# Where TensorE's tiles begin: stationary tiles moved to several distances, modulo 512 bytes, from their moving partners

## The chip, the cores and the metric

The kernel runs on one core of one Trainium2 chip. The metric is the device time of the whole launch in microseconds (us), the median of several runs. TensorE multiplies, VectorE (DVE), ScalarE (ACT) and GpSimd (POOL) do the elementwise work, SyncE (SP) and ScalarE's queue issue most transfers, and 16 DMA engines move the data.

## What is computed

One block of an encoder for 512 tokens of width 1024, in float32. A mixer comes first, then a retrieval layer over 16,384 experts, then a norm. Cut to what matters:

```python
h = rmsnorm(x, g_mix); z = h @ w_in
a = pool_mixer(z_pool) @ w_branch_pool
b = short_conv_mixer(z_c, z_b, z_v) @ w_branch_conv
x = x + (sigmoid(gate_a) * a + sigmoid(gate_b) * b) @ w_out
h2 = rmsnorm(x, g_ffn); q = h2 @ w_q
# per token and head: the best 16 of 128 x 128 sums of two key scores, softmax over the 16
act = gelu(expert_u[idx] . h2)
x = x + sum_k gate_k * act_k * expert_v[idx_k]
out = rmsnorm(x, g_final)
```

## The kernel before, in words

Every product of TensorE is made of three matmuls: each float32 operand is split into a high part (rounded to the `F32R` type, by ScalarE) and a low part (the rest, by VectorE or GpSimd), and high times high, high times low and low times high are summed (`mm3`, lines 57 to 60). Each matmul has its own load of 128 x 128 stationary elements, which TensorE makes while the matmul before it streams its moving operand.

The stages follow one another. **Mixer**: `w_in` comes in 16 pieces of 1 MB (`w_load`, line 181; tile `raw`), each is split into `wh` and `wl` in the pool `wpool`, and multiplies `hH` and `hL`, the normed and transposed input (`z_part`, line 210); then the branches and `w_out`. **Queries and keys**: eight heads (`queries`, `best_keys`, `top16`), with VectorE finding the best keys. **Expert gates**: for 320 of the 512 tokens the layer is computed densely, for all 128 blocks of 128 experts: `u_mm` (line 453) multiplies one block's `uH` and `uL` (stationary) with `h2H` and `h2L` (moving, 320 columns) in 24 matmuls; blocks 0 to 75 are done ahead, beside the queries and beside the building of a gate matrix from one-hot tiles `oi` and `oj` (line 865), which goes through memory (`Gd`, from the tile `stage`). The other tokens gather their experts' rows one by one (`gather`, tile `gr`), two VectorE passes over each. **Values**: for each block `weigh` (line 886) multiplies the activations (`a`, or `ab` when they come back from memory) with the gates `gt` and splits the result into `wH` and `wL`, and `v_part` (line 905) uses these as stationary operands against the moving `vH` and `vL`, in 18 matmuls of 512 columns; the last 52 blocks do their `u_mm` in the same loop (lines 966 to 990).

The order is written out by hand, and tiles stand in SBUF where pools put them: a pool's tiles stand one behind the other in the order in which they are first asked for, left pools upwards, right ones (`side="right"`) downwards. Tile sizes alone thus set the byte in a partition at which each tile begins. In the kernel before, all that TensorE reads begins at a multiple of 512 bytes: `hH`, `hL` (and `h2H`, `h2L`, which take their place), `uH`, `uL`, `vH`, `vL`, `wH`, `wL`, `wh`, `wl`, `mH`, `mL`, `oi`, `oj`. Slices of them along a partition (`wH[:, ts]`, `uH[:, c]`) step by whole multiples of 512 bytes too. The gates `gt[:, :, k]` of the four blocks of one load, read by VectorE and ScalarE, begin 128 bytes apart. Three lines show how a tile's size serves this:

```python
warm = edge.tile([P, 120], F32, name="warm")
rank0 = keep.tile([P, 48], F32, name="rank0")[:, :TOPK]
us[i] = [upool.tile([P, DC, P], F32R, tag=f"u{x}{i % 3}", name=f"u{x}", bufs=1) for x in "HL"]
```

`u_load`, `u_high` (lines 435 to 443) keep three blocks of u in turn (`i % 3`), `weigh` three of `wH` and of `wL`.

Of the kernel before, what the change touches and what calls it, by code (L numbers as in the profile page):

```python
# [8 lines left out]
F32 = mybir.dt.float32  # L9
F32R = mybir.dt.float32r  # L10
I32 = mybir.dt.int32
U32 = mybir.dt.uint32
# [4 lines left out]
P = 128  # L17
D = 1024
T = 512
NT = T // P  # L20
DC = D // P
H = 8
TOPK = 16
# [7 lines left out]
TD = KD * P  # L31
# [16 lines left out]
def block_kernel(ctx: ExitStack, tc: tile.TileContext, io, out, dbg=None):  # L48
# [27 lines left out]
        work.tile([P, 5, 1], F32, tag="rms", name="st", bufs=3)  # L76
    keep = ctx.enter_context(tc.tile_pool(name="keep", bufs=1))
    edge = ctx.enter_context(tc.tile_pool(name="edge", bufs=1, side="right"))
    warm = edge.tile([P, 120], F32, name="warm")
    pscale = keep.tile([P, 4], F32, name="pscale")  # L80
    cw = keep.tile([P, 12], F32, name="cw")
    rank0 = keep.tile([P, 48], F32, name="rank0")[:, :TOPK]
# [236 lines left out]
    for hf in range(2):  # L319
        us = []  # L320
# [25 lines left out]
        for e in range(2):  # L346
            zb = z_chunk(wb, e)
            p = fpool.tile([P, T], F32, tag="p", name="yb", bufs=2)
# [10 lines left out]
    for hf in range(4):  # L359
# [14 lines left out]
        for e in range(2):  # L374
# [3 lines left out]
            m = fpool.tile([P, T], F32, tag="p", name="m", bufs=2)  # L378
            t = fpool.tile([P, T], F32, tag="s", name="t", bufs=2)
# [44 lines left out]
    upool = tc.alloc_tile_pool(name="upool", bufs=2, reuse_waits="tile")  # L424
    qpool = tc.alloc_tile_pool(name="qpool", bufs=1, reuse_waits="tile")
# [6 lines left out]
    raws, us, hid = {}, {}, {}  # L432
    nu = [0]

    def u_load(i):
        if i < NK:
            raws[i] = upool.tile([P, DC, P], F32, tag=f"ur{i % 3}", name="ur", bufs=1)
            nc.sync.dma_start(raws[i], io["expert_ut"][i])

    def u_high(i):  # L440
        if i < NK:
            us[i] = [upool.tile([P, DC, P], F32R, tag=f"u{x}{i % 3}", name=f"u{x}", bufs=1) for x in "HL"]
            nc.scalar.copy(us[i][0], raws[i])  # L443

    def u_low(i, eng):
# [3 lines left out]
    def u_split(i, eng):  # L449
        u_high(i)  # L450
        u_low(i, eng)
# [18 lines left out]
    def u_tick(n=1, eng=nc.gpsimd, half=None):  # L470
        for _ in range(n):
            i = nu[0]
            nu[0] += 1
            u_load(i + 3)
            u_high(i + 2)
            if eng is not None:
                u_low(i + 2, eng)
            u_act(i, u_mm(i, half))
# [12 lines left out]
    for i in range(3):  # L491
        u_load(i)
# [16 lines left out]
    nc.sync.dma_start(skT, io["sub_keys_t"])  # L509

    nc.vector.tensor_scalar(rank0, iota[:, :TOPK], 2.0, 1.0, op0=ALU.mult, op1=ALU.max)
    ones = qpool.tile([P, NT * TOPK], U32, name="ones")
    nc.vector.memset(ones, 1)
    thirty = qpool.tile([P, NT * TOPK], U32, name="thirty")
    nc.vector.memset(thirty, 30)
# [314 lines left out]
    for n in range(0, TD // 4, 2):  # L830
# [14 lines left out]
        i = nu[0]  # L845
        nu[0] += 1
        u_load(i + 3)
        u_high(i + 2)
        one_hots(n + 2)
        one_hots(n + 3)  # L850
# [24 lines left out]
    epool = tc.alloc_tile_pool(name="epool", bufs=2, reuse_waits="tile")  # L875
# [10 lines left out]
    def weigh(i):  # L886

        if i < NK:
            a = abs_.pop(i) if i < n_ahead else hid.pop(i)
            g = gts.pop(i)  # L890
            gu = g[:, :TU // TG]
            nc.vector.tensor_tensor(gu, a.rearrange("p (n t) -> p n t", t=TG), gu, ALU.mult)  # L892
            wH = epool.tile([P, TD], F32R, tag="wH", name="wH", bufs=3)
            wL = epool.tile([P, TD], F32R, tag="wL", name="wL", bufs=3)
            nc.scalar.copy(wH.rearrange("p (n t) -> p n t", t=TG), g)  # L895
            ws[i] = (wH, wL, g)
# [52 lines left out]
    for k in range(U_END):  # L949
        u_tick(1, nc.vector)  # L950
        gather(n_done[0] + 2, 2)
        if k == 0:
            v_high(0)
            v_low(0)
        if k == 1:
            v_high(1)
            v_low(1)
        if k == U_END - 2:
            weigh(0)
            weigh_low(0)  # L960
# [5 lines left out]
    for i in range(NK - 1):  # L966
# [14 lines left out]
        if i < NK - 3:  # L981
            v_mm(i)
        weigh(i + 1)
        first = n_done[0] + 1
        for k in range(n_done[0], want):
# [85 lines left out]
```

## Time and profile before

| | |
|---|---|
| runs shown | 1512.49, 1513.56, 1513.67 us; median 1513.56 us |
| profiled execution | 1516.77 us, its span 1515.0 us, mean granted TensorE clock 0.993 |
| TensorE matmul busy | 1465.3 us, 97% of the span |
| TensorE weight load busy | 1291.0 us, 85% |
| VectorE busy | 1223.0 us, 81% |
| ScalarE, GpSimd busy | 668.8 and 653.8 us, 44% and 43% |
| DMA | 415.72 MB, mean 274 GB/s |

Busy time is the union of the durations that the trace gives. The end of a matmul is modelled, so that successive matmuls overlap in it: their rate is read from the distance between their starts, not from their durations. An instruction's "idle before" is the time for which its engine had nothing running, with the event that ended it. The granted clock is in parts of the higher of TensorE's two levels.

### The profile page before, as it was taken

The numbers are of one execution on the slowest core, as the hardware profiler recorded it, in microseconds if no ns is written. First come the engines' busy times: TensorE is split into PE (matmuls) and PEld (weight loads), VectorE is DVE, ScalarE is ACT, GpSimd is POOL, SyncE is SP. The second block draws the span as 40 slices with busy tenths as digits, with TensorE's granted clock in tenths as the row PEclk, the third lists the DMA queues.
The fourth block names the chain that finished last, engine by engine and source line by source line (L and its number), as shares of the span: only waits on it lengthen the run. The fifth ranks groups of instructions, "written<-read, shape, count | busy, mean of one in ns | idle before, by whom it ended". The sixth has DMA issues, their size and how long they took to land.

```text
span 1515.0 us, 22211 instructions
## 1 busy us (share of the span) xinstructions
PE 1465.3 (97%) x7953; PEld 1291.0 (85%) x7953; DVE 1223.0 (81%) x2399; ACT 668.8 (44%) x1144; POOL 653.8 (43%) x432
## 2 busy tenths in 40 slices
PE   8999999999998999999999999999999999999997
PEld 6788888788897989898997788888889999999996
DVE  5842434659999899999988888888889999999975
ACT  4323223423333677776853334333343343334334
POOL 3433333247772454544243243332345655555510
PEclk9999999999999999999999999999999999999999
DMA  5222224432224899999999999999999999999951
GB/s 188 83 98 83 97 87 159 125 130 102 110 74 136 301 392 363 373 376 387 363 323 396 346 352 377 363 349 376 360 376 368 381 393 364 405 375 380 372 221 70
DMA packets 163358, 415.72 MB, mean 274 GB/s; under 512 B 13744, under 2 KB 80304, under 8 KB 156848
## 3 DMA queue, kind: packets, MB, share of 16 engines
q1 hardware_dynamic: 102992, 210.99, 38.7%
q0 software_dynamic: 46144, 167.80, 28.9%
q10 hardware_dynamic: 14112, 35.53, 6.0%
q8 instruction: 62, 1.02, 0.3%
q14 instruction: 48, 0.39, 0.1%
HBM read 376.05 MB, written 37.62 MB: 273 GB/s over the span
## 4 chain that ended last, share of the span: by engine, by line
PE 66%; DVE 24%; issue 4%; DMA 4%; ACT 2%; POOL 0%; DVEq 0%; ACTq 0%; SPq 0%; POOLq 0%
PE b L911 30%; PE b L60 11%; PE b L59 11%; PE b L58 11%; DVE gr L731 5%; DMA ab<-Ad 3%; DVE uL L447 2%; DVE oj L812 2%; DVE oi L812 2%; PE b L865 1%; DVE oj L823 1%; DVE key L610 1%; DVE eq L596 1%; DVE sc L530 1%; DVE ti L528 1%
## 5 line engine op out<-in xcount | busy, mean ns | idle before, releaser
L60 PE MATMUL b<-h2H,uL 128*128 128x320 f32 x1024 | 321.7, 314 | 19.1 <-DVE uL L447 18.7
L58 PE MATMUL b<-h2H,uH 128*128 128x320 f32 x1024 | 322.5, 315 | 0.2 <-ACT h2H L54 0.2
L59 PE MATMUL b<-h2L,uH 128*128 128x320 f32 x1024 | 317.9, 310 | 0.9 <-DVE h2L L55 0.9
L719 POOL DMA_INDIRECT gr<-in_expert_u,gidx x128 | 172.7, 1349 | 242.8 <-DVE dots L731 147.6
L719 POOL DMA_INDIRECT gr<-in_expert_v,gidx x128 | 164.9, 1288 | 199.5 <-DVE x L736 119.8
L911 PE MATMUL b<-vH,wH 128*128 128x512 f32 x768 | 238.5, 391 | 5.2 <-ACT wH L895 5.2
L911 PE MATMUL b<-vH,wL 128*128 128x512 f32 x768 | 238.2, 391 | 0.0
L911 PE MATMUL b<-vL,wH 128*128 128x512 f32 x768 | 237.5, 390 | 0.0
L60 PEld LDWEIGHTS b<-h2H,uL 128*128 128x128 f32 x1024 | 193.7, 189 | 27.7 <-DVE uL L447 27.7
L880 ACT CAST vH<-vr 128x1024 fp32r<-128x1024 f32 x128 | 134.7, 1052 | 172.3 <-PE b L911 120.0
L884 DVE TENSOR_TENSOR vL<-vr,vH 128x1024 fp32r<-128x1024 f32 x128 | 156.7, 1224 | 60.1 <-ACT vH L880 59.4
L59 PEld LDWEIGHTS b<-h2L,uH 128*128 128x128 f32 x1024 | 194.0, 189 | 3.1 <-DVE h2L L55 1.2
L58 PEld LDWEIGHTS b<-h2H,uH 128*128 128x128 f32 x1024 | 194.2, 190 | 2.5 <-ACT h2H L54 0.5
L911 PEld LDWEIGHTS b<-vH,wL 128*128 128x128 f32 x768 | 143.2, 188 | 32.5 <-DVE wL L902 2.8
L911 PEld LDWEIGHTS b<-vL,wH 128*128 128x128 f32 x768 | 144.2, 188 | 30.8
L911 PEld LDWEIGHTS b<-vH,wH 128*128 128x128 f32 x768 | 141.5, 188 | 33.6 <-ACT wH L895 7.6
L736 DVE SCALAR_TENSOR_TENSOR x<-gr,dots,x 128x1024 f32<-128x1024 f32 x128 | 163.8, 1280 | 1.0
L731 DVE CUSTOM_DVE_ANT_0 gr<-gr,hn 128x1024 f32<-128x1024 f32 x128 | 153.8, 1218 | 2.0 <-DMA gr<-in_expert_u,gidx 2.0
L443 ACT CAST uH<-ur 128x1024 fp32r<-128x1024 f32 x128 | 133.9, 1047 | 35.4 <-ACT a L464 19.6
L447 DVE TENSOR_TENSOR uL<-ur,uH 128x1024 fp32r<-128x1024 f32 x113 | 139.5, 1236 | 8.1 <-ACT uH L443 8.1
L55 POOL TENSOR_TENSOR wl<-raw,wh 128x2048 fp32r<-128x2048 f32 (+1 forms) x21 | 79.5, 3784 | 150.6 <-ACT wh L54 150.6
L895 ACT CAST wH<-gt 128x384 fp32r<-128x384 f32 x128 | 65.8, 514 | 175.3 <-DVE gt L892 175.3
(216 smaller groups left out, 2487.3 us busy)
## 6 DMA issues: line engine op xcount, KB each, us to landing
ur<-in_expert_ut SPq DMA_DIRECT2D x128, 512.0 KB, 7.1
vr<-in_expert_v SPq DMA_DIRECT2D x128, 512.0 KB, 6.6
Gd<-stage ACTq DMA_DIRECT2D x22, 1024.0 KB, 9.0
gt<-Gd SPq DMA_DIRECT2D x32, 704.0 KB, 9.5
raw<-in_w_in SPq DMA_DIRECT2D x15, 1024.0 KB, 4.8
Ad<-a ACTq DMA_DIRECT2D x76, 160.0 KB, 5.7
ab<-Ad SPq DMA_DIRECT2D x76, 160.0 KB, 8.1
raw<-in_w_q SPq DMA_DIRECT2D x8, 1024.0 KB, 6.7
```

The source lines that it names most:

```text
L55: (nc.gpsimd if pool else nc.vector).tensor_tensor(Ld, src, f(Hd), ALU.subtract)
L58: nc.tensor.matmul(o, lh, rh, start=first, stop=False)
L59: nc.tensor.matmul(o, lh, rl, start=False, stop=False)
L60: nc.tensor.matmul(o, ll, rh, start=False, stop=last)
L443: nc.scalar.copy(us[i][0], raws[i])
L447: eng.tensor_tensor(us[i][1], raws.pop(i), f(us[i][0]), ALU.subtract)
L719: nc.gpsimd.indirect_dma_start(out=r, out_offset=None, in_=io["expert_u" if kind == "u" else "expert_v"], in_offset=bass.IndirectOffsetOnA ...
L731: nc.vector.tensor_tensor_reduce(out=r, in0=r, in1=src, op0=ALU.mult, op1=ALU.add, scale=1.0, scalar=0.0, accum_out=dst)
L736: nc.vector.scalar_tensor_tensor(x1[:, KD + g], r, dots[:, g, k:k + 1], x1[:, KD + g], op0=ALU.mult, op1=ALU.add)
L880: nc.scalar.copy(vs[i][0], vraw[i])
L884: nc.vector.tensor_tensor(vs[i][1], vraw.pop(i), f(vs[i][0]), ALU.subtract)
L911: nc.tensor.matmul(acc[tb][hf], lw[:, ts], rw[:, hf * 512:(hf + 1) * 512], start=i == 0 and rw is vH and lw is wH, stop=last and i == NK - 1)
```

## The change

Six tiles get other sizes or places, and nothing else changes. A helper `room` gives a u tile some elements behind its 1,024, which moves the tiles behind it: `ur` of the third block, `uL` of the first and of the second are 64, 64 and 128 bytes longer. `wH` is 320 bytes longer than its 384 elements. `ones`, 256 bytes, leaves `qpool` for the pool `edge` at the right end, where `warm` shrinks from 480 to 32 bytes: the right pools move by 192 bytes.

```diff
-    warm = edge.tile([P, 120], F32, name="warm")
+    warm = edge.tile([P, 8], F32, name="warm")
+    ones = edge.tile([P, NT * TOPK], U32, name="ones")
...
+    def room(tag, name, dt, more):
+
+        t = upool.tile([P, D + more], dt, tag=tag, name=name, bufs=1)
+        return t[:, :D].rearrange("p (c m) -> p c m", c=DC)
+
     def u_load(i):
         if i < NK:
-            raws[i] = upool.tile([P, DC, P], F32, tag=f"ur{i % 3}", name="ur", bufs=1)
+            raws[i] = room(f"ur{i % 3}", "ur", F32, 16 if i % 3 == 2 else 0)
             nc.sync.dma_start(raws[i], io["expert_ut"][i])
...
-            us[i] = [upool.tile([P, DC, P], F32R, tag=f"u{x}{i % 3}", name=f"u{x}", bufs=1) for x in "HL"]
+            us[i] = [room(f"u{x}{i % 3}", f"u{x}", F32R, (16, 32, 0)[i % 3] if x == "L" else 0) for x in "HL"]
             nc.scalar.copy(us[i][0], raws[i])
...
-    ones = qpool.tile([P, NT * TOPK], U32, name="ones")
     nc.vector.memset(ones, 1)
...
-            wH = epool.tile([P, TD], F32R, tag="wH", name="wH", bufs=3)
+            wH = epool.tile([P, TD + 80], F32R, tag="wH", name="wH", bufs=3)[:, :TD]
```

Where the tiles begin, in bytes modulo 512, as the two programs place them, and the distance from the moving to the stationary one (all were 0 before, but for `a`):

| tile | after | its partner in TensorE, after | distance |
|---|---|---|---|
| `uH`, `uL`, blocks 0, 1, 2 of three | 64, 128, 256 | `h2H`, `h2L`: 0 | 64, 128, 256 |
| `wH`, three buffers | 256, 64, 384 | `vH`, `vL`: 256 | 0, 320, 128 |
| `wL`, three buffers | 192 | `vH`: 256 | 448 |
| `wh`, `wl` (and `raw`) | 192 | `hH`, `hL`, `h2H`, `h2L`, `pH`, `yH`: 0; in `w_out` they move against `mH`, `mL`: 0 | 192; 320 |
| `oi`, `oj` | 256 | each other | 0 |
| `skT` | 256 | `q`: 0 | 256 |
| `gr`, `vr`, `gt`, `ab` (0 before) | 256 | not read by TensorE | |
| `stage` (0 before) | 192 | not read by TensorE | |
| `a`, three buffers (0, 256, 0 before) | 256, 0, 256 | not read by TensorE | |

On all five engines the instructions stand in the same order as before, with the same waits, but for one place on VectorE, at the beginning of the queries (`thirty` is a second table of constants, `tv` the best scores). Before:

```order
L511 TENSOR_SCALAR rank_73<-iota 128x16
L513 MEMSET ones 128x64 [waits Pool_49]
L515 MEMSET thirty 128x64
L526 MAX tv<-sc 128x8 [waits Activation_49]
```

and with the change, where the lines' numbers are higher by four or five:

```order
L517 TENSOR_SCALAR rank_74<-iota 128x16
L518 MEMSET ones 128x64
L520 MEMSET thirty 128x64 [waits Pool_49]
L531 MAX tv<-sc 128x8 [waits Activation_49]
```

The wait for GpSimd moved from the first constant to the second, which stands right behind it.

## Rows read from the trace of the kernel before

**Rows 1.** The page: span, and busy time, share and instructions of each engine.

```profile
span 1515.0 us, 22211 instructions
PE 1465.3 (97%) x7953; PEld 1291.0 (85%) x7953; DVE 1223.0 (81%) x2399; ACT 668.8 (44%) x1144; POOL 653.8 (43%) x432
```

**Rows 2.** Stretches of the span, busy time and instructions of each engine.

```profile
core 0: us, PE busy (x) PEld busy (x) DVE busy (x) ACT busy (x) POOL busy (x), PEclk, DMA share, GB/s
0.00:300.00 300.00, 289.83 (x1324) 237.15 (x1324) 146.49 (x193) 100.72 (x125) 102.40 (x39) 0.99 0.33 112
300.00:500.00 200.00, 188.25 (x1064) 170.53 (x1065) 175.72 (x900) 71.75 (x107) 114.91 (x74) 0.97 0.32 116
500.00:800.00 300.00, 282.00 (x2033) 272.90 (x2031) 287.30 (x492) 212.70 (x498) 138.76 (x91) 0.99 0.97 366
800.00:1100.00 300.00, 298.54 (x1305) 243.65 (x1306) 250.51 (x350) 117.77 (x166) 99.15 (x86) 1.00 1.00 364
1100.00:1400.00 300.00, 300.00 (x1652) 271.21 (x1652) 277.34 (x352) 119.22 (x172) 171.63 (x124) 1.00 1.00 380
1400.00:1515.00 115.00, 106.64 (x580) 95.59 (x578) 85.69 (x117) 46.65 (x77) 26.98 (x20) 0.98 0.59 223
```

**Rows 3.** The chain that ended last, by engine and by line.

```profile
PE 66%; DVE 24%; issue 4%; DMA 4%; ACT 2%; POOL 0%; DVEq 0%; ACTq 0%; SPq 0%; POOLq 0%
PE b L911 30%; PE b L60 11%; PE b L59 11%; PE b L58 11%; DVE gr L731 5%; DMA ab<-Ad 3%; DVE uL L447 2%; DVE oj L812 2%; DVE oi L812 2%; PE b L865 1%; DVE oj L823 1%; DVE key L610 1%; DVE eq L596 1%; DVE sc L530 1%; DVE ti L528 1%
```

**Rows 4.** Timeline of TensorE in the mixer: start, duration, instruction.

```profile
149.77 0.39 PE L58 MATMUL b<-hH,wh 128*128 128x512 f32 x1
...
152.95 0.39 PE L60 MATMUL b<-hH,wl 128*128 128x512 f32 x1
```

**Rows 5.** Timeline of TensorE in the values stage, two matmuls a row.

```profile
899.75 0.62 PE L911 MATMUL b<-vL,wH 128*128 128x512 f32 x2
900.21 0.62 PE L911 MATMUL b<-vH,wL 128*128 128x512 f32 x2
...
902.92 0.62 PE L911 MATMUL b<-vH,wL 128*128 128x512 f32 x2
```

**Rows 6.** Timeline of matmuls (PE) and weight loads (PEld) in one block of u.

```profile
1205.82 0.31 PE L59 MATMUL b<-h2L,uH 128*128 128x320 f32 x1
1205.82 0.19 PEld L60 LDWEIGHTS b<-h2H,uL 128*128 128x128 f32 x1
...
1205.97 0.31 PE L60 MATMUL b<-h2H,uL 128*128 128x320 f32 x1
...
1208.31 0.31 PE L58 MATMUL b<-h2H,uH 128*128 128x320 f32 x1
```

**Rows 7.** Timeline of VectorE: the multiplications by the gates, four blocks in turn.

```profile
903.13 0.48 DVE L892 TENSOR_TENSOR gt<-ab,gt 128x320 f32<-128x320 f32 x1
...
907.21 0.49 DVE L892 TENSOR_TENSOR gt<-ab,gt 128x320 f32<-128x320 f32 x1
...
911.29 0.49 DVE L892 TENSOR_TENSOR gt<-ab,gt 128x320 f32<-128x320 f32 x1
...
915.33 0.49 DVE L892 TENSOR_TENSOR gt<-ab,gt 128x320 f32<-128x320 f32 x1
```

**Rows 8.** The page: the values stage's matmuls, busy, mean ns, idle before.

```profile
L911 PE MATMUL b<-vH,wH 128*128 128x512 f32 x768 | 238.5, 391 | 5.2 <-ACT wH L895 5.2
...
L911 PE MATMUL b<-vL,wH 128*128 128x512 f32 x768 | 237.5, 390 | 0.0
```

**Rows 9.** The page: DMA queue of ScalarE, and issues with median us to landing.

```profile
q10 hardware_dynamic: 14112, 35.53, 6.0%
...
Gd<-stage ACTq DMA_DIRECT2D x22, 1024.0 KB, 9.0
...
raw<-in_w_in SPq DMA_DIRECT2D x15, 1024.0 KB, 4.8
```

## The prediction

> **What bounds the kernel now.** I read the busy shares first [rows 1]: TensorE is busy for 97% of the span, and no other engine comes near. An average hides stages, so the table by stretch comes next [rows 2]. The reader should see three kinds of stretch there. From 0 to 300 us (the mixer) TensorE is busy for 290 of 300 us while VectorE has half its time free. From 300 to 800 us (queries, then the building of the gates) VectorE is the fuller one: 176 of 200 us and 287 of 300 us. From 800 us on (values) TensorE has no gap left, 298.5 and 300 of 300 us, VectorE has 250 and 277, and the DMA engines show a share of 1.00. The chain that ended last [rows 3] agrees: 66% of it is TensorE, and 24% VectorE.
>
> So what the change can do to the time, it must do to the rate at which TensorE takes matmuls in the stretches from 0 to 300 us and from 800 us to the end. These hold 1324 + 1305 + 1652 + 580 = 4861 matmuls [rows 2]. In the stretch between, a little more or less per matmul is covered by VectorE, and it counts only if VectorE itself changes.
>
> The rate is read from starts. In the mixer 14 matmuls of 512 columns lie between 149.77 and 152.95 us: 227.1 ns each [rows 4]. In the values stage 14 lie between 899.75 and 902.92 us: 226.4 ns [rows 5]. In a block of u, 17 of 320 columns lie between 1205.82 and 1208.31 us: 146.5 ns [rows 6]. [...]
>
> **The change, part by part.**
>
> The order of instructions and the waits are the same, but for one wait for GpSimd that goes from the first of two neighbouring constants on VectorE to the second. Nothing stands between the two and nobody waits for the first alone; cost 0.
>
> No operation is added, removed or made larger: the longer tiles are used through views of their old size. ScalarE and VectorE read and write as many elements as before; cost 0, unless where a tile begins matters to them. For VectorE the trace shows that it hardly does. The gates of four successive blocks begin 128 bytes apart, so VectorE reads its two operands at distances of 0, 128, 256 and 384 bytes modulo 512 in turn. The multiplications of four such blocks take 0.48, 0.49, 0.49 and 0.49 us [rows 7]. If two streams at distance 0 hindered each other there, one block in four would stand out.
>
> For TensorE no row shows another distance than 0, so its price must be bounded. Not every matmul changes its distance. One of the three `wH` buffers still meets `vH` and `vL` at 0: of 768 + 768 matmuls with `wH` [rows 8] that is a third, 512; in the mixer about 100 more (the half of `w_out` that stands in the place of `pHL` and `yHL`) keep theirs. That leaves about 4250 of the 4861. [...] The nearest row is the one in which an engine reads two streams at several distances, VectorE's, and it says 0. There is a second reason for a value near 0. Between 149 and 153 us the DMA engines are a third busy and VectorE half idle; at 900 us there are 364 GB/s of transfers and a nearly full VectorE, all of them on the same memory. TensorE's rate is the same, 227.1 against 226.4 ns [rows 2, 4, 5]. Foreign accesses at all sorts of addresses do not show in it. I take **0 ns per matmul**.
>
> [...]
>
> The transfers move too. `gr`, `vr`, `gt` and `ab` begin at 256 instead of 0, `stage` and `raw` at 192. `raw` is loaded in the mixer, where the DMA share is 0.33, 4.8 us for 1 MB, two pieces ahead [rows 2, 9]: hidden even at twice the time. `stage` is read for `Gd` in the gate stretch, where the DMA share is 0.97; that is rival C. The rest I cost at 0. What hides it if it is a little more than that is the issue ahead of need (blocks are loaded two to three ahead); without that cover, a slower gather would show as VectorE waiting for `gr`.
>
> Sum: 0 + 0 + 0 = 0 us. Against the profiled execution of 1516.8 us that is 1516.8 us, which stands 3.2 us above the median of the runs; I give the forecast against the median: **1513.5 us**. A measurement of this kernel tells about 0.2%, 3 us, from no change.
>
> **The rivals.**
>
> [...]
>
> *B, slower: another distance costs what 0 does not.* Two streams that begin together at the same residue may part at once and never meet; one that begins 64, 128 or 256 bytes ahead may be caught while it is still being read, and then one of them waits. The place is the same two kinds of stretch. It decides as soon as a matmul of 512 columns starts over 0.7 ns later than now (3 us over 4250). For: that all distances are 0 now and the rate is steady. [...]
>
> *C, slower: the transfers of `stage`.* 22 writes of 1 MB land in 9.0 us each, in a stretch that is already full of transfers; ScalarE's queue, which holds these writes, takes 6.0% of the engines' span, 91 us [rows 9]. A tenth more, half of it exposed: 4.5 us, **1518 us**. Against: VectorE bounds that stretch, not the transfers. [...]
>
> *The change may not do what it says* for the first `wH` buffer (distance 0) and the one-hots; this is in the count above and makes a control: these matmuls must start as far apart as now.
>
> **How the numbers follow.** No change: 0.56, with 1510.5 to 1516.5 us as its own range. A: 0.23. B: 0.16, C: 0.05. So faster 0.23, same 0.56, slower 0.21. For 8 in 10 the range must take in somewhat over half of A and B: down to 5.5 ns per matmul (24 us), and as far up: **1490 to 1537 us**.
>
> **What would show it.** In the profile after: TensorE's starts in the mixer (distance 192), in u's blocks by turns of three (64, 128, 256) and in the values stage by turns of three for `wH` and for `wL`. If I am right they are 226 to 227 and 146 to 147 ns in all of these. One distance that stands out by over a nanosecond would make the prediction wrong by 5 us or less at a single set of tiles, more if all stand out. VectorE's multiplications by gates staying at 0.48 to 0.49 us would hold its step; the writes of `Gd` landing in clearly over 9.0 us would be C.

## The result, and the profile after

The changed kernel takes 1524.9 us (median of four runs, 1524.47 to 1526.01) against 1513.6 us before: 0.72% longer, 95% interval 0.54% to 0.89%. The profiled execution took 1526.0 us with a span of 1524.2 us, 9.2 us more than the span before.

The page of the changed kernel, span and engines:

```profile
span 1524.2 us, 22211 instructions
PE 1477.7 (97%) x7953; PEld 1294.0 (85%) x7953; DVE 1223.6 (80%) x2399; ACT 669.1 (44%) x1144; POOL 654.8 (43%) x432
```

As many instructions as in [rows 1]; VectorE, ScalarE and GpSimd are busy for as long as before, to 1 us. TensorE alone is busy for 12.4 us more.

Where in the program the time is lost is read from first and last starts of a line's instructions. The view of one line or tile gives count, shortest, median and longest duration in ns, and first and last start. The last matmuls of the mixer (`w_out`) and those of the values, before:

```profile
L58 PE MATMUL b<-yHL,mH x16: 389/389/389, 268.1 to 288.3; 128*128 128x512 f32 x16
L911 PE MATMUL b<-vH,wH x768: 389/389/505, 793.5 to 1505.8; 128*128 128x512 f32 x192
```

and after:

```profile
L58 PE MATMUL b<-yHL,mH x16: 389/389/389, 270.4 to 290.6; 128*128 128x512 f32 x16
L916 PE MATMUL b<-vH,wH x768: 387/393/628, 795.0 to 1515.0; 128*128 128x512 f32 x192
```

(L916 is the line that was L911; it has other numbers again in the edited kernels below.) The mixer ends 2.3 us later. The values stage begins 1.5 us later, so that a part of this is made up in between, and it lasts 7.7 us longer (720.0 for 712.3 us). That is the whole difference.

The values stage in the timeline of the changed kernel, the rows with which a block of 18 matmuls begins (`wH` at distance 128, 320, 0, then 128 again, `wL` always at 448):

```profile
903.37 0.62 PE L916 MATMUL b<-vH,wH 128*128 128x512 f32 x2
...
907.52 0.63 PE L916 MATMUL b<-vH,wH 128*128 128x512 f32 x2
...
911.71 0.62 PE L916 MATMUL b<-vH,wH 128*128 128x512 f32 x2
...
915.87 0.62 PE L916 MATMUL b<-vH,wH 128*128 128x512 f32 x2
```

The three blocks take 4.15, 4.19 and 4.16 us: 230.6, 232.8 and 231.1 ns a matmul, where [rows 5] gave 226.4. Even the block whose `wH` stands at distance 0 is slower; its `wL` stands at 448, and the run with `wL` alone, below, shows that `wL`'s place is enough to slow a block (230.9 ns with `wL` at 64, 233.6 at 128). No wait stands in these rows. The mixer's matmuls, now at distance 192, and u's at 128:

```profile
149.85 0.39 PE L58 MATMUL b<-hH,wh 128*128 128x512 f32 x1
...
153.28 0.39 PE L58 MATMUL b<-hH,wh 128*128 128x512 f32 x1
```

```profile
1203.99 0.31 PE L58 MATMUL b<-h2H,uH 128*128 128x320 f32 x1
...
1207.36 0.31 PE L60 MATMUL b<-h2H,uL 128*128 128x320 f32 x1
```

Fifteen steps in the mixer make 3.43 us, 228.7 ns each [rows 4: 227.1]; 23 steps in u make 3.37 us, 146.5 ns each, as in [rows 6]. Over all of u's matmuls with neighbours of the same kind the means are 146.7, 146.7 and 146.6 ns at 64, 128 and 256, and 146.6 ns at 0 in the kernel before.

The stretches after, to be set against [rows 2] (same columns):

```profile
500.00:800.00 300.00, 284.90 (x2051) 275.84 (x2049) 288.47 (x497) 213.44 (x499) 138.38 (x90) 0.99 0.96 364
800.00:1100.00 300.00, 298.39 (x1282) 241.73 (x1283) 248.03 (x347) 116.16 (x165) 98.81 (x86) 0.99 0.99 360
1100.00:1400.00 300.00, 300.00 (x1631) 268.51 (x1630) 274.49 (x348) 117.92 (x170) 169.39 (x123) 1.00 0.99 376
```

From 800 to 1400 us TensorE is as full as before (298.39 and 300.00 us), at a granted clock of 0.99 and 1.00 where it had 1.00 and 1.00, and takes 2913 matmuls instead of 2957. VectorE and the transfers have less to do per time, not more. No new wait shows: the same instructions on the same engine start further apart.

### The profile page after: what moved, and what is told of

Its sections match the earlier page's. It is cut to its first block, busy times and chain, and to the rows that moved or that the text cites. A ratio compares the mean times of both kernels' runs of the same rounds, so it can differ in the third digit from the quotient of the medians.

```text
span 1524.2 us, 22211 instructions
## 1 busy us (share of the span) xinstructions
PE 1477.7 (97%) x7953; PEld 1294.0 (85%) x7953; DVE 1223.6 (80%) x2399; ACT 669.1 (44%) x1144; POOL 654.8 (43%) x432
## 4 chain that ended last, share of the span: by engine, by line
PE 72%; DVE 22%; issue 4%; ACT 1%; DMA 0%; POOL 0%; DVEq 0%; SPq 0%; ACTq 0%; POOLq 0%
PE b L916 35%; PE b L60 12%; PE b L59 12%; PE b L58 11%; DVE gr L736 4%; DVE oj L817 2%; DVE uL L453 2%; DVE oi L817 2%; PE b L870 2%; DVE oj L828 1%; DVE key L615 1%; DVE eq L601 1%; DVE sc L535 1%; DVE ti L533 1%; DVE ti L539 1%
## 5 line engine op out<-in xcount | busy, mean ns | idle before, releaser
L916 PE MATMUL b<-vH,wH 128*128 128x512 f32 x768 | 240.2, 393 | 3.8 <-ACT wH L900 3.8
L916 PE MATMUL b<-vL,wH 128*128 128x512 f32 x768 | 241.7, 395 | 0.0
L916 PE MATMUL b<-vH,wL 128*128 128x512 f32 x768 | 241.6, 396 | 0.0
L916 PEld LDWEIGHTS b<-vH,wL 128*128 128x128 f32 x768 | 144.6, 189 | 34.5 <-DVE wL L907 0.5
L916 PEld LDWEIGHTS b<-vL,wH 128*128 128x128 f32 x768 | 144.4, 188 | 33.1
L916 PEld LDWEIGHTS b<-vH,wH 128*128 128x128 f32 x768 | 142.3, 188 | 33.6 <-ACT wH L900 4.5
L724 POOL DMA_INDIRECT gr<-in_expert_u,midx x64 | 99.8, 1559 | 96.8 <-DVE mdots L736 83.3
```

Source lines behind the costliest of these rows:

```text
L724: nc.gpsimd.indirect_dma_start(out=r, out_offset=None, in_=io["expert_u" if kind == "u" else "expert_v"], in_offset=bass.IndirectOffsetOnA ...
L916: nc.tensor.matmul(acc[tb][hf], lw[:, ts], rw[:, hf * 512:(hf + 1) * 512], start=i == 0 and rw is vH and lw is wH, stop=last and i == NK - 1)
```

## The experiments

All are the kernel before with one thing edited, unless said otherwise. Times and ratios stand against runs of the kernel before on the same chip (1515.6 us median for the first four, 1515.8 us for the next four, a single run of 1516.2 us for the last three). The "excess" of the expectations is an estimate: by [rows 4, 5, 6], 192 columns more make a matmul 79.9 to 80.6 ns longer, 0.42 ns a column, and a straight line through these starts leaves 12.2 to 13.3 ns per matmul beside the columns.

**u's tiles alone.** The helper `room` and the longer u tiles of the change; `ones` and `warm` share the 480 bytes of `edge`, and a tile of 256 bytes ahead of the gathers' buffers puts everything behind u back to 0.

```diff
+        t = upool.tile([P, D + more], dt, tag=tag, name=name, bufs=1)
...
+    gpool.tile([P, 64], F32, name="shift")
```

> Only u's tiles are moved (uH and uL at 64, 128 and 256 bytes, distances 64, 128, 256 to h2H and h2L at 0); everything of the values stage and of the mixer begins at 0 as before. Theory D (the distance between stationary and moving tile costs time): the profile of the change shows u's matmuls at 146 to 147 ns at all three distances, so 0 us, 1512 to 1516 us. A theory by which any distance costs as much per matmul as the values stage lost (4 to 5 ns) would give about 1250 matmuls in the open x 4.5 ns = 6 us more.

Measured: 1515.8 us, ratio 1.0003, interval 0.9994 to 1.0012. u's part of the change, and with it the moved wait, costs nothing that these runs show.

**`wH` alone.**

```diff
-            wH = epool.tile([P, TD], F32R, tag="wH", name="wH", bufs=3)
+            wH = epool.tile([P, TD + 80], F32R, tag="wH", name="wH", bufs=3)[:, :TD]
```

> Only wH is 320 bytes longer: wH at 0, 320, 128, wL at 448, vH and vL stay at 0. The distances are those of the change, 0, 320, 128 and 448; the moving tiles begin at a multiple of 512. Theory D (the distance counts): the whole loss comes back, +9 to +12 us, 1523 to 1526 us, and the 512-column matmuls of the values stage start 231 to 232 ns apart on average. Rival R (what counts is that the moving tile itself does not begin at a multiple of 512 bytes): 0 us, 227 ns.

Measured: 1523.9 us, ratio 1.0059, interval 1.0046 to 1.0073. The blocks of the values stage (distance 128, then 320, then 0 begins):

```profile
901.90 0.62 PE L911 MATMUL b<-vH,wH 128*128 128x512 f32 x2
...
906.05 0.63 PE L911 MATMUL b<-vH,wH 128*128 128x512 f32 x2
...
910.24 0.62 PE L911 MATMUL b<-vH,wH 128*128 128x512 f32 x2
```

4.15 and 4.19 us again, with `vH` and `vL` at 0. No tile but `wH` and `wL` begins elsewhere than in the kernel before. One line makes most of the loss.

**The mixer's side alone.**

```diff
-    warm = edge.tile([P, 120], F32, name="warm")
+    warm = edge.tile([P, 72], F32, name="warm")
```

> Only the right pools are moved by 192 bytes: wh, wl, raw and stage at 192, the rest at 0 as before. Theory D: the mixer's matmuls at distance 192 lose 2 ns each as in the profile of the change, 1.5 to 2.5 us by the end of the mixer, most of it won back where VectorE bounds; total 0 to +2 us. Rival C (the transfers of stage, which no longer begins at a multiple of 256 bytes, slow the stretch in which the gates are built): +4 us or more, with Gd landing in clearly over 9 us.

Measured: 1518.4 us, ratio 1.0020, interval 1.0011 to 1.0029. The same views as above, and the writes of `Gd` and loads of `raw` (count, KB each, median us to landing):

```profile
L58 PE MATMUL b<-yHL,mH x16: 389/389/389, 270.5 to 290.7; 128*128 128x512 f32 x16
L911 PE MATMUL b<-vH,wH x768: 387/389/628, 795.3 to 1509.6; 128*128 128x512 f32 x192
```

```profile
Gd<-stage ACTq DMA_DIRECT2D x22, 1024.0 KB, 7.3
...
raw<-in_w_in SPq DMA_DIRECT2D x15, 1024.0 KB, 4.8
```

The mixer ends 2.4 us later than before and the values begin 1.8 us later; the rest of the 2.8 us is not attributed (the values' matmuls start 227 ns apart, and single executions of the kernel before lie between 1512.4 and 1518.0 us). `Gd` lands in 7.3 us, where [rows 9] had 9.0 (8.1 to 8.8 in other runs with `stage` at 0), and `raw` in 4.8 as there. Rival C does not happen. Of my expectation, the 2 ns per matmul came; that most of it would be won back did not.

**The values' tiles moved together.**

```diff
+    gpool.tile([P, 64], F32, name="shift")
     dots = upool.tile([P, NT - KD, P], F32, name="dots", bufs=1)
```

> A tile of 256 bytes ahead of the gathers' buffers moves gr, vr, gt, ab, oi, oj, vH, vL, wH and wL by 256 bytes together: distances in TensorE stay 0, but each of these tiles begins at 256. Theory D: 0 us, 227 ns a matmul. Rival R (the moving tile's own place counts): +9 to +12 us, 231 to 232 ns. A rival by which the gathers or the loads of v at 256 cost time would show as VectorE waiting for gr, with TensorE's starts at 227 ns.

Measured: 1515.4 us, ratio 1.0002, interval 0.9993 to 1.0011. One block:

```profile
899.70 0.62 PE L912 MATMUL b<-vH,wH 128*128 128x512 f32 x2
...
903.77 0.62 PE L912 MATMUL b<-vH,wH 128*128 128x512 f32 x2
```

4.07 us, 226.1 ns a matmul, with every tile at 256. A common shift of 256 bytes costs nothing, nor do the gathers at 256. Rival R falls, here and in the run with `wH` alone, where the moving tiles stood at 0 and the loss came back. But 256 bytes turn out, below, to be a whole period, so that this run does not tell the distance from the place of the stationary tile alone.

The four together: 0.03 + 0.59 + 0.20 + 0.02 = 0.84% for the parts, 0.72% (0.54 to 0.89) for the change.

**Sweeps of the distance.** `wH` and `wL` of one block get the same distance, another one for each of the three buffers, and the mixer's tiles one of their own. The edit of `wH` and `wL` for the first of three kernels (which moves u too; the lines that move u and the mixer's tiles are left out here):

```diff
+            j = i % 3
+            if i == 0:
+                epool.tile([P, 8], F32, name="shift", bufs=1)
-            wH = epool.tile([P, TD], F32R, tag="wH", name="wH", bufs=3)
-            wL = epool.tile([P, TD], F32R, tag="wL", name="wL", bufs=3)
+            wH = epool.tile([P, TD + (0, 0, 0)[j]], F32R, tag=f"wH{j}", name="wH", bufs=1)[:, :TD]
+            wL = epool.tile([P, TD + (8, 16, 0)[j]], F32R, tag=f"wL{j}", name="wL", bufs=1)[:, :TD]
```

> Distance sweep, all tiles of one block at one distance: wH and wL at 32, 64 and 128 by turns of three with vH, vL at 0; u at 32, 96, 192; the mixer's wh, wl at 64. Theory D1 (0 is the best distance, any other costs a 512-column matmul 2 to 8 ns): each of the three v distances over 228 ns on average, the total +4 to +12 us. Rival D2 (part of the excess is a collision at distance 0, which some distance avoids): at least one distance under 226 ns. Rival D3 (a uniform distance costs nothing, only different distances within one block's wH and wL do): 227 ns in all three, 0 us. u at 146 to 147 ns in all three.

> The same sweep at 192, 256 and 320 for wH and wL, u at 0, the mixer's wh, wl at 256. D1: over 228 ns at each, 229 at 192 as the mixer showed at 192, and the total +4 to +12 us. D2: some distance under 226 ns. D3: 227 ns in all, 0 us (against it: the mixer at 192, uniform, took 229 ns).

> The same sweep at 384, 448 and 480 for wH and wL, u at 0, the mixer's wh, wl at 384. D1: over 228 ns at each, the total +4 to +12 us. D2: some distance under 226 ns. D3: 227 ns in all, 0 us.

Measured: 1534.0 us (1.0126, interval 1.0109 to 1.0143), 1521.7 us (1.0041, 1.0027 to 1.0056) and 1530.3 us (1.0092, 1.0075 to 1.0109). Beginnings of blocks at 128, 32, 64, and the next, in the first:

```profile
899.84 0.63 PE L920 MATMUL b<-vH,wH 128*128 128x512 f32 x2
...
904.03 0.63 PE L920 MATMUL b<-vH,wH 128*128 128x512 f32 x2
...
908.23 0.63 PE L920 MATMUL b<-vH,wH 128*128 128x512 f32 x2
...
912.43 0.62 PE L920 MATMUL b<-vH,wH 128*128 128x512 f32 x2
```

at 256, 320, 192, and the next, in the second:

```profile
899.21 0.62 PE L914 MATMUL b<-vH,wH 128*128 128x512 f32 x2
...
903.31 0.63 PE L914 MATMUL b<-vH,wH 128*128 128x512 f32 x2
...
907.51 0.63 PE L914 MATMUL b<-vH,wH 128*128 128x512 f32 x2
...
911.64 0.62 PE L914 MATMUL b<-vH,wH 128*128 128x512 f32 x2
```

A block takes 4.19, 4.20, 4.20 us at 128, 32, 64, and 4.10, 4.20, 4.13 us at 256, 320, 192, where it took 4.07 to 4.08 at 0. Means over all matmuls of 512 columns, from the third of a block on and without the few steps that hold a wait, in ns:

| distance | 0 | 32 | 64 | 128 | 192 | 256 | 320 | 384 | 448 | 480 |
|---|---|---|---|---|---|---|---|---|---|---|
| values | 227.1 | 233.3 | 233.4 | 232.8 | 229.0 | 227.7 | 233.4 | 232.7 | 228.9 | 233.3 |
| mixer | 226.9 | | 233.3 | | 228.9 | 226.8 | | 233.3 | | |

The row repeats after 256 bytes: 64 is as 320, 128 as 384, 192 as 448, and 256 as 0 (the 0.6 ns in the values are the first matmuls of a block, which come from another distance; later ones stand at 227). D1 holds in its sign, but with a period of 256 and not 512, and the totals of the first and third kernel, 18 and 15 us more, lie above its 4 to 12; D2 and D3 fall for 512 columns: none is quicker than 0, and a uniform distance costs as much as a mixed one. u's matmuls of 320 columns take 146.7 ns at each of 32, 96 and 192.

In all of this table the moving tile begins at a multiple of 256 bytes, so "distance" could as well be the stationary tile's own place. Only the first 96 matmuls of `w_out` can tell the two apart, for there `wh` and `wl` move and `mH` and `mL` stand at 0. In the first kernel of the sweep, `wh` and `wl` at 64, so that the distance is 448:

```profile
259.26 0.40 PE L58 MATMUL b<-wh,mH 128*128 128x512 f32 x1
...
262.76 0.40 PE L58 MATMUL b<-wh,mH 128*128 128x512 f32 x1
```

Fifteen steps make 3.50 us, 233.3 ns each. The mean is also 233.3 with `wh` and `wl` at 192 (the change) and at 384, and 226.7 with them at 0 and at 256. So it is not the stationary tile's place alone, which is the same in all of these. Nor is it the distance alone: 448 cost 229 ns in the table and costs 233 here. What all the runs bear is narrower: at 512 columns 227 ns with both tiles at a multiple of 256 bytes, 229 to 233 with one of them off it.

One group went the other way. The mixer's first matmuls have 256 columns. They take 119.6 to 119.8 ns at 0 and 256, 118.6 at 384, 117.8 at 192 and 114.6 at 64.

**`wL` alone.** The same edit with `wH` always at 0, `wL` at 64, 128, 256.

> wH at 0 in all three buffers, wL at 64, 128 and 256 by turns: two distances within one block. D1: the four of six loads that are of wH cost nothing, the two of wL 2 to 8 ns: about a third of the loss of a uniform distance, +2 to +4 us. D3: the mixture itself costs, 231 ns on average as in the run that lengthened wH alone, +8 us or more.

Measured: 1521.4 us (1.0040, interval 1.0026 to 1.0054). The means of a block are 230.9, 233.6 and 228.1 ns for `wL` at 64, 128, 256. Neither expectation fits: a third of the loads at a distance costs over half of what all of them cost (at 64 bytes 3.8 ns a matmul of 6.3), and with `wL` at 128 the block costs as much as with both there. A matmul's own pair does not settle its time; within such blocks matmuls of `wH` at distance 0 that load the next `wH`, at 0 as well, take up to 236 ns.

**The width of the moving tile.** One run each: u with 512 and with 384 columns in the last 52 blocks, and the values in pieces of 256 columns with `wH` and `wL` at 0, 64, 128. The columns added to u are computed and not used.

```diff
-            mm3(o[:, :TU], uH[:, c], uL[:, c], h2H[:, c, :TU], h2L[:, c, :TU], c == 0, c == DC - 1)
+            w = 512 if i >= n_ahead else TU
+            mm3(o[:, :w], uH[:, c], uL[:, c], h2H[:, c, :w], h2L[:, c, :w], c == 0, c == DC - 1)
```

> u's tiles at 64, 128 and 256 as in the change, all else at 0; the 52 blocks of u in the values stage move 512 columns instead of 320 (the 192 more are not used). So the time is longer by 52 x 24 x 80 ns = 100 us, and only the starts count. Theory W (the distance counts or not by the moving tile's width, whichever tiles they are): 233 ns at 64, 233 at 128, 227 at 256, as wH and wL showed at 512 columns. Rival U (u's tiles are free of it for another reason, such as loads of other slices each time): 227 ns at all three.

> The same with 384 columns (64 more than are used): 160 ns of columns and 13 of excess, 173 ns where the distance costs nothing, 52 x 24 x 27 ns = 34 us longer in all. Theory W: at 64 and 128 something between what 320 columns showed (0 ns) and 512 (+6 ns) if the effect grows with the width; 256 bytes at 173 ns as at a distance of 0.

```diff
+                for q in (0, 256):
+                    nc.tensor.matmul(acc[tb][hf][:, q:q + 256], lw[:, ts], rw[:, hf * 512 + q:hf * 512 + q + 256],
...
```

> Every matmul of the values stage is cut in two of 256 columns, with wH and wL at 0, 64 and 128 by turns; twice as many matmuls and loads of weights, so the time is longer by 2304 x (2 x 120 - 227) ns = 30 us, and the starts count. Theory W: at 256 columns a distance of 64 is the quicker one, 113 to 115 ns against 120 at 0, as the first matmuls of the mixer showed; 128 in between at 118 to 119. Rival U: 120 ns at all three.

Blocks of u with 512 columns, at 256 and then at 64: the first matmul of each, and the first behind its 24.

```profile
1315.86 0.39 PE L58 MATMUL b<-h2H,uH 128*128 128x512 f32 x1
...
1321.30 0.62 PE L918 MATMUL b<-vH,wH 128*128 128x512 f32 x2
...
1325.38 0.40 PE L58 MATMUL b<-h2H,uH 128*128 128x512 f32 x1
...
1330.98 0.62 PE L918 MATMUL b<-vH,wH 128*128 128x512 f32 x2
```

5.44 us at 256 is 226.7 ns a matmul, 5.60 us at 64 is 233.3; the mean at 128 is 232.4. The tiles that were indifferent at 320 columns are as sensitive at 512 as any other. At 384 columns the means are 174.7 ns at 64, 176.1 at 128, 174.7 at 256: 1.5 ns at most. And the values in pieces of 256 columns, 32 steps each at 64 and at 0:

```profile
902.65 0.63 PE L913 MATMUL b<-vH,wH 128*128 128x256 f32 x4
...
906.41 0.64 PE L913 MATMUL b<-vH,wL 128*128 128x256 f32 x4
...
911.17 0.64 PE L913 MATMUL b<-vH,wH 128*128 128x256 f32 x4
...
915.01 0.64 PE L913 MATMUL b<-vH,wL 128*128 128x256 f32 x4
```

117.5 ns at 64 here (115.9 in the mean of all such blocks, in two groups: 117.8 up to 1108 us, but for the first of them, and 113.4 from 1128 us on, where each follows a block of u), 120.0 at 0; 118.8 at 128. The times of these three runs, 1619.3, 1553.1 and 1534.3 us, carry the added work; the last is 12 us under the 30 us more that I had expected, of which the quicker matmuls at 64 and 128 make 8 us (1512 x 4.1 ns and 1584 x 1.2 ns); the rest is not attributed. W holds and U falls: what the distance costs depends on the width.

No version that beats both kernels came out of this. At 512 columns 0 is already the best of ten distances, u does not care, and two matmuls of 256 columns at 64 take 2 x 115.9 = 232 ns for one of 227 (2 x 113.4 = 227 in the quicker group, no gain either).

## Why the prediction was wrong

It forecast no change, 1513.5 us, with 1510.5 to 1516.5 us as that outcome's own range, and gave rival B, slower, 0.16. B is what happened, at 1524.9 us; the stated range of 1490 to 1537 us holds it, because it reaches 5.5 ns per matmul to either side. That 5.5 ns was an estimate of mine, and no run shows it as a bound: at 512 columns, with one of the tiles off a multiple of 256 bytes, the means lie 1.8 to 6.6 ns above those at distance 0, and none lies below. Step by step:

**The stage that sets the time** was right: what the change did, it did through TensorE's rate in the mixer and from 800 us on, and nothing else moved. The moved wait, the longer tiles and the transfers cost nothing that shows, as said: the run with u's tiles alone holds the wait and the longer u tiles, those with the mixer's side alone and with the values' tiles moved together hold every moved transfer, and rival C is refuted by its own number, `Gd` in 7.3 us. In the traces of the two kernels the median piece of 8 KB of these writes took 309 ns with `stage` at 192 and 309 ns with `stage` at 0.

**The step that failed is the price per matmul**, "I take 0 ns", and the two reasons under it. The first was VectorE's multiplications by the gates at four distances [rows 7]. They are still alike after the change (478 to 493 ns, median 485, for 482 to 493, median 484), so the reading of the row was right, but it says nothing of TensorE: at the distances 128 and 384, which are among VectorE's four, TensorE loses close to 6 ns a matmul of 512 columns (232.8 and 232.7 for 227.1). The second was that foreign transfers and a busy VectorE leave TensorE's rate alone [rows 4, 5]. That is so too (227.1 and 226.4 ns), but the two streams that count are TensorE's own: between the kernel before and the run with `wH` alone, the same instructions at 227 and at 231 to 233 ns differ only in the addresses of `wH` and `wL`. I had taken the evidence of other readers of the memory for the one pair that the trace held at a single distance.

**Rival B** was right in kind: another distance costs what 0 does not. The cost is 4.5 ns a matmul in the 76 blocks of values that stand alone (4167 ns a block for 4086, sums of medians, mean over the three buffers) and 3.6 ns in the 52 that follow a block of u (4172 for 4107): 76 x 81 + 52 x 65 ns = 9.5 us. The profile shows 7.7 us of it; waits for `wH` fall from 5.2 to 3.8 us, and the rest is not attributed. In the mixer it is 2 ns, and 6.6 ns in the 96 matmuls of `w_out` whose distance changes; together 2.3 us by its end, 1.5 us by the start of the values. For u it is 0 to 0.1 ns (146.6 and 146.7 for 146.6), which I could not have read from the trace of the kernel before. The control that I named, the first `wH` buffer at distance 0, was none: its blocks took 231 ns, since a neighbour's distance counts as well, as the run with `wL` alone shows.

**The faster outcome**, A, given 0.23, falls for 512 columns: no distance brings the mean under the 227 ns that it is at 0. At 256 columns there is one, 64 bytes, that takes 2 to 6 ns off (113.4 to 117.8 for 119.7 to 120.0). So an address can make a matmul quicker than distance 0 does, but not the matmuls that fill this kernel.

What stays open: why. The experiments show that the time of a matmul depends on where its two tiles begin relative to each other modulo 256 (227 to 233 ns at 512 columns) and on the width (at 256 columns 113 to 120 ns, quickest at 64), and that it follows from the sequence of pairs rather than from one pair (up to 236 ns for a pair at distance 0 beside others). Whether the distance alone counts is not settled, and `w_out` at 64 speaks against it; no run has both tiles at the same place other than a multiple of 256 bytes. What passes between the two streams of reads, if anything does, no run shows.

## What to carry to other kernels

For a chain of matmuls of 512 float32 columns, each with its own load of weights, the layout to keep is the one in which stationary and moving tiles both begin at a multiple of 256 bytes: it took 227 ns a matmul here, every other layout tried 229 to 233, 1 to 3% more, and a longer tile in front of one that TensorE reads is enough to lose it (`wH` longer by 320 bytes: 8.3 us, 0.59%). At 320 columns the distance made 0.1 ns (146.6 and 146.7) and at 384 at most 1.5 ns (174.7 to 176.1); at 256 columns that layout was the slowest of those tried, 119.6 to 120.0 ns for 113.4 to 118.8. A layout like this is worth one line in a profile: read starts of matmuls, not their durations (means of 390 and 391 ns before and 393 to 396 after for the values' matmuls, whose starts lie 227 and 230 to 233 ns apart), before and after any edit that changes a tile's size.

## What the runs showed of the hardware that I had not expected

- With the moving tile at a multiple of 256 bytes, the start-to-start time of a matmul with its own weight load depends on the distance to the stationary one with a period of 256 bytes: at 512 float32 columns 227 ns at 0 and 256, 229 at 192 and 448, 233 at 32, 64, 128, 320, 384 and 480. With the stationary tile at 0 and the moving one at 64, 192 or 384 it is 233 ns.
- The sign depends on the width: at 64 bytes 6 ns more at 512 columns (233.3 and 233.4 for 226.7 to 227.1), 0 to 0.1 at 320 and 384 (146.7 for 146.6, 174.7 for 174.7), 2 to 6 ns less at 256 (113.4 to 117.8 for 119.7 to 120.0).
- The pattern within a block is steady and repeats (226, 229, 232 ns at 192 bytes; in the values at 128 every seventh step takes 241), and in a block of mixed distances pairs at distance 0 are slowed too, up to 236 ns.
- VectorE's multiplications by the gates, with their two operands at any of four distances, take the same 0.48 to 0.49 us (128 x 320 float32).
